# Values of units 1 and 2 in one pass of 512 columns, branch A's last gate group between units 2 and 3, the mixing's products on GpSimd

## The chip, the cores and the metric

The kernel runs on one core of a Trainium2 chip. The metric is the device time of one execution in microseconds (us). The kernel before takes 898.06 us, the median of three runs (897.68 to 898.46).

## What is computed

One layer of a hybrid decoder on a sequence of 512 tokens with 2048 features, then a final RMSNorm, in fp32.

```python
def reference(x, c, norm_g, w_ada, b_ada, w_in, ln_v_g, ln_v_b, w_s, b_s, b_f, w_out, final_g):
    cond = jax.nn.silu(c)
    ...
        shift, scale, gate = jnp.split(mod, 3, axis=-1)
        h = rms_norm(x, norm_g[l]) * (1.0 + scale[:, None, :]) + shift[:, None, :]
        z = h @ w_in[l]
        u_a, v_a, g_a, q_b, k_b, v_b, g_b, f_b = jnp.split(z, pts, axis=-1)
        y_a = chunked_spatial_gating(jax.nn.gelu(u_a, approximate=False),
                                     jax.nn.gelu(v_a, approximate=False),
                                     ln_v_g[l], ln_v_b[l], w_s[l], b_s[l]) * jax.nn.silu(g_a)
        y_b = forgetting_attention(q_b, k_b, v_b, f_b, b_f[l]) * jax.nn.silu(g_b)
        y = jnp.concatenate([y_a, y_b], axis=-1) @ w_out[l]
        x = x + gate[:, None, :] * y
    return rms_norm(x, final_g)
```

`z` has 7184 columns: 1024 each for u, v and gate of branch A and for q, k, v and gate of branch B, and 16 forget logits. Branch A normalises v and mixes it over the tokens: 8 heads, each with a lower triangular 128x128 matrix on chunks of 128 tokens. Branch B is causal attention of 16 heads of 64, whose scores have the running sum of log-sigmoid forget gates added.

## The kernel before

**Engines.** PE (TensorE) multiplies; DVE (VectorE), ACT (ScalarE) and POOL (GpSimd) do the rest; SP issues most loads. A framework orders each engine's instructions ahead of time, from the order of the code and from priorities; each engine then runs its own list strictly in order and waits on semaphores. A wait therefore holds up all that is queued behind it.

**Products.** Every fp32 operand is split into a high and a low part, and a product is three matmuls: high by high, low by high, high by low. Weights come in tiles (`w_tile`, L126 to L146): SP loads `raw` (4 buffers), ACT copies it to the high part `whi` (L141), DVE subtracts for the low part `wlo` (L145; 2 buffers each). Two forms of product use them:

- `mm_cols` (L163 to L165): 128 weight columns are stationary and 512 tokens move; used by q, k and the gates (`col_group`, L177). Names: q, k, ga (gates of A), gb (gates of B).
- `mm_toks` (L173 to L175): 128 tokens are stationary and the weight columns move; used by the values, va of branch A (512 columns at a time) and vb of branch B. `v_group` (L825) does one unit's 256 columns (272 in unit 0, with the forget logits).

**Units.** Branch B's heads are done in four units of four heads. Order of groups: va, ga (the last 256 columns of A's gates), v0, q0, k0, gb0, q1, k1, v1, gb2, q2, k2, v2, q3, k3, v3, gb1, gb3, then the output projection. A unit's values go to the tile `vs` as high and low parts right behind its pass (L66 on ACT, L67 on DVE).

**Ticks.** After each weight tile, `tick()` (L148) takes one entry of the list `slots` (branch A's mixing, then attention) and one of `fillers` (mostly `gate_step`, the output gate's products on POOL, L723 and L727). So the small work is spread among the matmuls by counting weight tiles. A unit's attention is eight slots: scores (2 slots), `lse`, then exps and products with the values.

- Scores (L589, L590) are matmuls; DVE adds the mask and takes the minimum (L591), ACT exponentiates (L595).
- `lse` (L602 to L613): ACT takes the logarithm, PE transposes (L607), ACT copies the result to `lt` (L609), SP writes it by four small copies into rows of the q tiles (L612). Then `pins.append([4, rows_in])`: the load of the fifth weight tile from there is issued only behind those copies. This tile is called the pinned tile below.
- `probs`: matmuls t (L629, L630), exps p on ACT (L633, with a table load ahead), split into pth (ACT, L66) and ptl (DVE, L67). `values`: matmuls o (L645) and evacuation (L653 to L655).

**Branch A's mixing.** `norm_half` (L885) normalises and splits va for four heads; `mix_head` (L898 to L919) mixes one head: eight matmuls into two banks (L907, L908), four `scalar_tensor_tensor` (STT below) on DVE into `mt` (L911, L916), and the product of `mt` with y (L919, on DVE). `evac_g` (L445) multiplies in A's gates (L442, L451). The list of slots: norm 0; mix 0, 1; mix 2, 3; norm 1; then mix 4, 5, 6, 7 one by one. The first four slots fall into ga, the others into v0.

**PSUM.** Banks of the kind "mm" (four) take the groups' sums; "x" takes turns on four more banks, for scores, t, o, mixing, transposes, and q0's two sums.

Of the kernel before, what the change touches and what calls it, by code (L numbers as in the profile page):

```python
# [23 lines left out]
U0, V0, G0, Q0, K0, VB0, GB0, F0 = 0, 1024, 2048, 3072, 4096, 5120, 6144, 7168  # L24
# [3 lines left out]
def trunk_kernel(  # L28
# [17 lines left out]
    nc = tc.nc  # L46
# [6 lines left out]
    act = ctx.enter_context(tc.tile_pool(name="act", bufs=KB))  # L53
# [5 lines left out]
    def bank(tag, name):  # L59
        if tag == "x":  # L60
            tag = "bbbc"[turn[0] % 4]
            turn[0] += 1
        return ps.tile([P, 512], F32, tag=tag, name=name, bufs={"mm": 4, "b": 3, "c": 1}[tag])

    def split(hi, lo, src, eng=None):
        a = nc.scalar.activation(hi, src, AF.Copy)  # L66
        return a, (eng or nc.vector).tensor_tensor(lo, src, hi.bitcast(F32), ALU.subtract)  # L67
# [193 lines left out]
    def ada_sums(q, i, ga):  # L261
# [5 lines left out]
        for j in range(2):  # L267
# [15 lines left out]
            else:  # L283
                for c_ in ((slice(0, P), slice(P, 2 * P)) if q == 0 and kk == KB - 2 else (slice(0, 256),)):
# [153 lines left out]
    y = [None] * KB  # L438

    def silu2(dst, pt):  # L440
        ta = nc.scalar.activation(dst, pt, AF.Tanh, scale=0.5)
        nc.vector.scalar_tensor_tensor(dst, dst, 1.0, pt, ALU.add, ALU.mult)  # L442
        return ta

    def new_y(b):  # L445
        y[b] = act.tile([P, S], F32, tag="ya" if b < 8 else "yb", bufs=8, name=f"y{b}")

    def evac_g(b, pt, pool):
        sg = pool.tile([P, S], F32, name=f"sgA{b}", tag="sgB", bufs=3 if pool is st else 4)
        ta = silu2(sg, pt)  # L450
        nc.vector.scalar_tensor_tensor(y[b], sg, 0.5, y[b], ALU.mult, ALU.mult)  # L451
        return ta

    for q, (k0, nk) in enumerate(CH):
# [10 lines left out]
        for si, sid in enumerate(order):  # L465
# [50 lines left out]
    pb = ctx.enter_context(tc.tile_pool(name="pb", bufs=1))  # L516
# [14 lines left out]
    vs_ = []  # L531
# [4 lines left out]
    def halves(e):  # L536
        return (slice(0, 64), slice(64, 128)) if e == 0 else (slice(64, 128), slice(0, 64))
# [257 lines left out]
    def spatial_weights():  # L795
# [10 lines left out]
        for i in range(2):  # L806
# [11 lines left out]
            for j in range(4):  # L818
# [3 lines left out]
                    bias2[:, h, :], ALU.mult, ALU.add,  # L822
                )

    def v_group(u):  # L825
        c0 = u * 256
        banks = [bank("mm", f"vb{u}_{t}") for t in range(NT)]
        segs, nk = ([(VB0 + c0, 256)], 4) if u else ([(VB0, 256), (F0, 16)], 2)
        w = sum(z for _, z in segs)
        for k in range(0, KB, nk):  # L830
            hi, lo = w_tile(segs, k, nk, name=f"vb{u}_{k}")
            mm_toks(banks, w, hi, lo, hh, hl, list(range(k, k + nk)), 0, KB - 1)
            tick()
        with tc.high_priority(offset=EPRI):
            for t in range(NT):
                src = banks[t][:, 0:256].rearrange("p (i d) -> p i d", d=64)
                for e in range(2):
                    a, o = halves(e)
                    split(vs_[0][:, t, e::2, a], vs_[0][:, t, e::2, o], src[:, e::2, :])
# [22 lines left out]
    c_ = lambda f, *a: (lambda: f(*a))  # L862
# [32 lines left out]
    def mix_head(h):  # L895
        g, j = divmod(h, 4)
        hs = slice(h * P, (h + 1) * P)
        js = slice(j * P, (j + 1) * P)  # L898
        mt = pb.tile([P, 512], F32, name=f"mt{h}", tag="p", bufs=2)
        b2 = bias2[:, h, :]  # L900
        w2 = wsp[h // 4][:, h % 4].rearrange("p a t -> p (a t)")
        for n in range(2):
            mx = bank("x", f"mix{h}_{n}")
            for i in range(2):
                vh, vl = vhl[2 * n + i, g]
                o = mx[:, i * 256 : (i + 1) * 256]
                nc.tensor.matmul(o, vh[:, js], w2, start=True, stop=False)  # L907
                nc.tensor.matmul(o[:, 0:P], vl[:, js], w2[:, 0:P], start=False, stop=True)  # L908
            m3 = mx.rearrange("p (n a t) -> p n a t", n=2, a=2)
            o3 = mt[:, n * 256 : (n + 1) * 256].rearrange("p (n t) -> p n t", n=2)  # L910
            nc.vector.scalar_tensor_tensor(  # L911
                o3, m3[:, :, 0, :], lngb[:, h : h + 1],
                bass.AP(tensor=b2.tensor, offset=b2.offset, ap=[b2.ap[0], [0, 2], b2.ap[1]]),
                ALU.mult, ALU.add,
            )
            nc.vector.scalar_tensor_tensor(  # L916
                o3, m3[:, :, 1, :], lngb[:, h : h + 1], o3, ALU.mult, ALU.add
            )
        nc.vector.tensor_tensor(y[h], y[h], mt, ALU.mult)  # L919

    fillers.append(spatial_weights)
    for k in range(8):
        fillers.extend([lambda k=k: sum_step(0, k), lambda: None])
    va_products()
    slots.extend([
        [c_(norm_half, 0)],
        [c_(mix_head, 0), c_(mix_head, 1)],
        [c_(mix_head, 2), c_(mix_head, 3)],
        [c_(norm_half, 1)],
        [c_(mix_head, 4)], [c_(mix_head, 5)], [c_(mix_head, 6)], [c_(mix_head, 7)],  # L930
    ])
    col_group([(G0 + 768, 256)], [(lambda pt, b=b: evac_g(b, pt, pb)) for b in range(6, 8)], "ga")
    vs_.append(pb.tile([P, NT, 4, P], F32R, name="vs", tag="vs"))
    v_group(0)
    heads_tiles()
# [17 lines left out]
    fillers.append(lambda: [f() for f in late_stores])  # L953
    qk_group(0)
    g_group(0)
    for u in range(1, 4):
        if u == 2:
            g_group(2)
        qk_group(u)
        v_group(u)  # L960

# [61 lines left out]
    def wtile(name):  # L1023
        return wp.tile([P, 2, 512], F32, tag="raw", name=name, bufs=4)
# [85 lines left out]
    def unit(u):  # L1110
# [3 lines left out]
        def w_raw(half, g, name):  # L1114
            return lambda i: wsplit(wget(wtile(f"{name}_{u}_{i}"), half, g, i), f"{name}_{u}_{i}")
# [6 lines left out]
            return f  # L1122

        def tiles(n, tag, b=2):
            pool = act if tag == "yb" else pb
            return [pool.tile([P, S], F32, name=f"{n}{u}_{t}", tag=tag, bufs=b) for t in range(2)]

        def evac(f):
# [6 lines left out]
                f(t)  # L1135

        product(V, "A11", w_raw(1, g1, "p1"), True)
        c1 = tiles("c1", "yb", 8) if u else tiles("c1", "th")
        evac(lambda t: nc.scalar.activation(c1[t], V[t], AF.Copy))
        Z = [bank("mm" if u else "x", f"woZ{u}_{t}") for t in range(2)]  # L1140
        product(Z, "S3", w_sum(1, "p7"), True)
        c7 = tiles("c7", "yb", 8) if u else tiles("c7", "p")
        evac(lambda t: nc.scalar.activation(c7[t], Z[t], AF.Copy))
        X = [bank("x", f"woX{u}_{t}") for t in range(2)]
        product(X, "S2", w_sum(3, "p6"), True)
        if u:
# [128 lines left out]
```

## Time and profile before

| | |
|---|---|
| median of three runs | 898.06 us (897.68 to 898.46) |
| the profiled execution | 899.12 us |
| its span in the trace | 897.4 us |
| granted clock of TensorE | 0.997 of full speed |
| PE, DVE, ACT, POOL busy | 98%, 68%, 50%, 53% of the span |

Where the groups start on PE, in us of the span: va 189.6, ga 279.4, v0 305.0, q0 333.5, k0 356.1, gb0 378.2, q1 405.1, k1 432.8, v1 461.3, gb2 493.5, q2 520.1, k2 547.5, v2 569.7, q3 598.6, k3 626.8, v3 653.0, gb1 681.7; the output projection runs from 735 to the end.

In rows of the timeline the first number is the start, the second the duration in us (both from the first instruction to the last of a group that stands under one row, with its count as x), then engine, line, operation, and out<-in; in brackets is the idle time of the engine just before, and what ended it. PE's matmuls are pipelined: a 512-column one lasts 0.39 us and the next starts 0.23 us after it, so steps from start to start tell PE's speed. In a table of stretches a row has the stretch, its length, busy time with the number of instructions of PE, PE's weight load, DVE, ACT and POOL, the granted clock, the DMA share and GB/s.

### The profile page before, as it was taken

The numbers are of one execution on the slowest core, as the hardware profiler recorded it, in microseconds if no ns is written. First come the engines' busy times: TensorE is split into PE (matmuls) and PEld (weight loads), VectorE is DVE, ScalarE is ACT, GpSimd is POOL, SyncE is SP. The second block draws the span as 40 slices with busy tenths as digits, with TensorE's granted clock in tenths as the row PEclk, the third lists the DMA queues.
The fourth block names the chain that finished last, engine by engine and source line by source line (L and its number), as shares of the span: only waits on it lengthen the run. The fifth ranks groups of instructions, "written<-read, shape, count | busy, mean of one in ns | idle before, by whom it ended". The sixth has DMA issues, their size and how long they took to land.

```text
span 897.4 us, 12688 instructions
## 1 busy us (share of the span) xinstructions
PE 881.7 (98%) x4453; PEld 744.7 (83%) x4453; DVE 614.7 (68%) x999; ACT 444.4 (50%) x778; POOL 479.7 (53%) x407
## 2 busy tenths in 40 slices
PE   9999999999999999999999999999999999999995
PEld 6788888887888897887889888998898888888884
DVE  5878888374427967563876664547664779997686
ACT  6653333452224224564656554556466567654454
POOL 1266554515676269999799779957566520000001
PEclk9999999999999999999999999999999999999998
DMA  9999996348986275544443536466666466577575
GB/s 340 354 352 355 354 344 205 111 134 284 331 285 200 61 212 155 156 139 136 142 150 117 187 107 188 129 193 198 222 188 211 165 214 200 174 263 244 178 245 195
DMA packets 123216, 188.91 MB, mean 211 GB/s; under 512 B 9856, under 2 KB 86864, under 8 KB 122640
## 3 DMA queue, kind: packets, MB, share of 16 engines
q1 hardware_dynamic: 113248, 153.97, 53.6%
q0 software_dynamic: 9472, 33.56, 11.6%
q8 instruction: 35, 0.57, 0.3%
q10 hardware_dynamic: 432, 0.57, 0.2%
q14 instruction: 29, 0.24, 0.1%
HBM read 166.90 MB, written 20.97 MB: 209 GB/s over the span
## 4 chain that ended last, share of the span: by engine, by line
PE 89%; DMA 4%; DVE 3%; ACT 1%; issue 1%; SPq 1%; POOLq 0%; POOL 0%; ACTq 0%
PE s L163 6%; PE s L165 6%; PE s L164 6%; PE k L165 3%; PE gb L164 3%; PE gb L165 3%; PE gb L163 3%; PE k L164 3%; PE k L163 3%; PE vb L173 3%; PE vb L174 3%; PE va L175 3%; PE va L174 3%; PE va L173 3%; PE vb L175 3%; PE q L165 3%
## 5 line engine op out<-in xcount | busy, mean ns | idle before, releaser
L723 POOL TENSOR_SCALAR gate<-gate,sc 128x512 f32<-128x512 f32 x64 | 108.5, 1708 | 1.4
L727 POOL TENSOR_TENSOR gate<-gate,gate 128x512 f32<-128x512 f32 x60 | 91.1, 1518 | 2.4
L145 POOL TENSOR_TENSOR wlo_st<-raw_st,whi_st 128x768 fp32r<-128x768 f32 (+3 forms) x33 | 66.0, 2001 | 45.0 <-ACT whi_st L141 39.8
L163 PE MATMUL s<-hh,whi_st 128*128 128x512 f32 x224 | 86.2, 391 | 0.9 <-ACT sp L501 0.9
L164 PE MATMUL s<-hl,whi_st 128*128 128x512 f32 x224 | 86.2, 389 | 0.0
L66 ACT ACTIVATE whi_p<-p 128x1024 fp32r<-128x1024 f32 x52 | 55.2, 1061 | 57.2 <-PE woZ L1059 22.1
L1102 POOL TENSOR_TENSOR sfin<-sfin,nhalf 128x1 f32<-128x1 f32 x2 | 1.5, 746 | 149.6 <-DVE sfin L1194 149.6
L285 DVE SCALAR_TENSOR_TENSOR acc<-ada,sc,acc 128x512 f32<-128x512 f32 x98 | 73.9, 754 | 6.2 <-DMA ada<-in_w_ada_dram 3.4
L67 DVE TENSOR_TENSOR wlo_p<-p,whi_p 128x1024 fp32r<-128x1024 f32 x52 | 63.4, 1221 | 19.6 <-ACT whi_p L66 19.5
L165 PE MATMUL s<-hh,wlo_st 128*128 128x512 f32 x224 | 75.3, 391 | 0.0
L173 PE MATMUL vb<-whi_vb,hh 128*128 128x256 f32 (+1 forms) x256 | 72.3, 285 | 0.8 <-DVE sgA L442 0.5
L174 PE MATMUL vb<-whi_vb,hl 128*128 128x256 f32 (+1 forms) x256 | 72.3, 285 | 0.0
L175 PE MATMUL vb<-wlo_vb,hh 128*128 128x256 f32 (+1 forms) x256 | 70.7, 284 | 0.0
L141 ACT ACTIVATE whi_st<-raw_st 128x768 fp32r<-128x768 f32 (+3 forms) x35 | 31.1, 890 | 68.6 <-PE s L164 49.3
L775 POOL TENSOR_TENSOR ts<-ts 128x256 f32<-128x256 f32 x64 | 57.0, 903 | 13.2 <-DMA ts<-in_w_out_dram 11.4
L67 DVE TENSOR_TENSOR ptl<-p,pth 128x512 fp32r<-128x512 f32 (+1 forms) x64 | 45.4, 733 | 14.1 <-ACT pth L66 13.0
L145 DVE TENSOR_TENSOR wlo_va<-raw_va,whi_va 128x1024 fp32r<-128x1024 f32 x16 | 24.6, 1538 | 39.3 <-ACT whi_va L141 39.3
L163 PEld LDWEIGHTS s<-hh,whi_st 128*128 128x128 f32 x224 | 42.0, 188 | 10.2 <-ACT sp L501 1.7
L163 PE MATMUL k<-hh,whi_k 128*128 128x512 f32 x128 | 50.4, 394 | 0.0
L163 PE MATMUL q<-hh,whi_q 128*128 128x512 f32 x128 | 50.4, 394 | 0.0
L164 PE MATMUL q<-hl,whi_q 128*128 128x512 f32 x128 | 50.4, 394 | 0.0
L173 PE MATMUL va<-whi_va,hh 128*128 128x512 f32 x128 | 50.3, 393 | 0.0
(317 smaller groups left out, 2628.0 us busy)
## 6 DMA issues: line engine op xcount, KB each, us to landing
ada<-in_w_ada_dram SPq DMA_DIRECT2D x128, 256.0 KB
gate<-in_w_ada_dram POOLq DMA_DIRECT2D x32, 512.0 KB, 4.4
p<-ts SPq DMA_DIRECT2D x32, 512.0 KB
p<-in_w_out_dram SPq DMA_DIRECT2D x24, 512.0 KB
raw_st<-in_w_in_dram SPq DMA_DIRECT2D x22, 384.0 KB
raw_va<-in_w_in_dram SPq DMA_DIRECT2D x16, 512.0 KB
raw_q<-in_w_in_dram SPq DMA_DIRECT2D x16, 512.0 KB
raw_k<-in_w_in_dram SPq DMA_DIRECT2D x16, 512.0 KB
```

The source lines that it names most:

```text
L67: return a, (eng or nc.vector).tensor_tensor(lo, src, hi.bitcast(F32), ALU.subtract)
L145: (loeng or nc.vector).tensor_tensor(lo, raw, hi.bitcast(F32), ALU.subtract)
L163: nc.tensor.matmul(pt, hi[:, j, cs], hh[k], start=(k == first), stop=False)
L164: nc.tensor.matmul(pt, hi[:, j, cs], hl[k], start=False, stop=False)
L165: newest = nc.tensor.matmul(pt, lo[:, j, cs], hh[k], start=False, stop=(k == last))
L173: nc.tensor.matmul(o, ah[k][:, tsl], hi[:, j, :], start=(k == first), stop=False)
L174: nc.tensor.matmul(o, al[k][:, tsl], hi[:, j, :], start=False, stop=False)
L175: nc.tensor.matmul(o, ah[k][:, tsl], lo[:, j, :], start=False, stop=(k == last))
L285: nc.vector.scalar_tensor_tensor((sb if kk == KB - 1 else a)[:, :, c_], ga[:, j, :, c_], col, a[:, :, c_], ALU.mult, ALU.add,)
L723: nc.gpsimd.tensor_scalar(ga[:, j] if kk else a, ga[:, j], sc[:, kk : kk + 1], None, ALU.mult)
L727: done = nc.gpsimd.tensor_tensor(a, a, ga[:, j], ALU.add)
L775: done = nc.gpsimd.tensor_tensor(dst, l, r, ALU.subtract)
```

## The change

Three edits, and the buffers that they need.

- **One pass of 512 columns.** `v_group(1)` loads the value columns of units 1 and 2 together, in 8 tiles of two row blocks each. Unit 1's half is split to `vs` as before; unit 2's half goes by ACT to two SBUF tiles `v2`, and `v_group(2)` only splits from those. Of the pools, y and the like lose two of eight buffers of the kind "yb" to a new kind "yc".
- **Gate group moved.** ga no longer stands ahead of v0 but between unit 2's values and q3. The list of the mixing is packed into v0's eight tiles. The groups' order becomes va, v0, q0, k0, gb0, v1 (with unit 2), q1, k1, gb2, q2, k2, ga, q3, k3, v3, gb1, gb3.
- **Products on GpSimd.** `y[h] * mt` goes from DVE (L919 before) to POOL (L940 after).

```diff
@@ v_group
+    def v_split(t, src):
+        src = src.rearrange("p (i d) -> p i d", d=64)
+        for e in range(2):
+            a, o = halves(e)
+            split(vs_[0][:, t, e::2, a], vs_[0][:, t, e::2, o], src[:, e::2, :])
...
+        if u == 2:
+            for t in range(NT):
+                v_split(t, v2[t // 2][:, t % 2 * 256 : t % 2 * 256 + 256])
+            return
         banks = [bank("mm", f"vb{u}_{t}") for t in range(NT)]
-        segs, nk = ([(VB0 + c0, 256)], 4) if u else ([(VB0, 256), (F0, 16)], 2)
+        segs, nk = {
+            0: ([(VB0, 256), (F0, 16)], 2), 1: ([(VB0 + c0, 512)], 2), 3: ([(VB0 + c0, 256)], 4),
+        }[u]
...
+                if u == 1:
+                    nc.scalar.activation(
+                        v2[t // 2][:, t % 2 * 256 : t % 2 * 256 + 256], banks[t][:, 256:512], AF.Copy
+                    )
@@ mix_head
-        nc.vector.tensor_tensor(y[h], y[h], mt, ALU.mult)
+        nc.gpsimd.tensor_tensor(y[h], y[h], mt, ALU.mult)
@@ slots
         [c_(norm_half, 0)],
-        [c_(mix_head, 0), c_(mix_head, 1)],
-        [c_(mix_head, 2), c_(mix_head, 3)],
-        [c_(norm_half, 1)],
-        [c_(mix_head, 4)], [c_(mix_head, 5)], [c_(mix_head, 6)], [c_(mix_head, 7)],
+        [c_(mix_head, 0)], [c_(mix_head, 1), c_(norm_half, 1)],
+        [c_(mix_head, 2), c_(mix_head, 3)], [c_(mix_head, 4)], [c_(mix_head, 5)], [c_(mix_head, 6)],
+        [c_(mix_head, 7)],
     ])
-    col_group([(G0 + 768, 256)], [(lambda pt, b=b: evac_g(b, pt, pb)) for b in range(6, 8)], "ga")
@@ the groups
     g_group(0)
-    for u in range(1, 4):
-        if u == 2:
-            g_group(2)
-        qk_group(u)
-        v_group(u)
+    v_group(1)
+    qk_group(1)
+    g_group(2)
+    qk_group(2)
+    v_group(2)
+    col_group([(G0 + 768, 256)], [(lambda pt, b=b: evac_g(b, pt, pb)) for b in range(6, 8)], "ga")
+    qk_group(3)
+    v_group(3)
```

Line numbers of the kernel after are higher: by 3 ahead of `v_group`, by 21 in the mixing. The attention slots of units 0 to 3 fall into gb0 and q1, v1 and gb2, v2 and q3, v3 and gb1 before; now into gb0 and v1, gb2 and q2, ga and q3, v3 and gb1.

The end of v0 on PE, before: the last matmuls of v0 (vb0_3, its tile 14), and the first of q0.

```order
L173 MATMUL vb0_3_2785<-whi_vb0_14_3070,hh15_1687 128x272
L174 MATMUL vb0_3_2785<-whi_vb0_14_3070,hl15_1688 128x272
L175 MATMUL vb0_3_2785<-wlo_vb0_14_3071,hh15_1687 128x272
L163 MATMUL q0_0_3150<-hh0_386,whi_q0_0_3154 128x512
L164 MATMUL q0_0_3150<-hl0_387,whi_q0_0_3154 128x512
```

The same place now. mix4_1 to mix7_1 are banks of the mixing of heads 4 to 7, and vh and vl the parts of va.

```order
L175 MATMUL vb0_3_2551<-wlo_vb0_14_2925,hh15_1687 128x272
L929 MATMUL mix4_1_2819<-wsp1_1892,vl3_1_2714 128x128
L929 MATMUL mix5_1_2866<-wsp1_1892,vl3_1_2714 128x128
L928 MATMUL mix6_0_2906<-wsp1_1892,vh0_1_2698 128x256
...
L929 MATMUL mix7_1_2960<-wsp1_1892,vl3_1_2714 128x128
L163 MATMUL q0_0_3020<-hh0_386,whi_q0_0_3024 128x512
```

The last piece of heads 4 and 5 and all of heads 6 and 7 stand between v0 and q0 (16 matmuls from mix6_0 to mix7_1). The banks take turns, and q0_0 gets mix6_0's.

DVE at that place, before: the parts of the values (vs) and the low parts of q0's weights.

```order
L145 TENSOR_TENSOR wlo_q0_0_3155<-raw_q0_0_3152,whi_q0_0_3154 128x1024
L67 TENSOR_TENSOR vs_2781<-vb0_0_2782,vs_2781 128x2x64
L67 TENSOR_TENSOR vs_2781<-vb0_1_2783,vs_2781 128x2x64
L67 TENSOR_TENSOR vs_2781<-vb0_2_2784,vs_2781 128x2x64
L67 TENSOR_TENSOR vs_2781<-vb0_0_2782,vs_2781 128x2x64
L145 TENSOR_TENSOR wlo_q0_4_3219<-raw_q0_4_3216,whi_q0_4_3218 128x1024
```

Now, from the first STT that reads mix4_1 (one more split of values stands behind it, and an STT of mix5_1) to the one that reads mix6_0 for the second time:

```order
L932 SCALAR_TENSOR_TENSOR mt5_2858<-mix5_1_2866,cols_128,bias2_1904 128x256
L937 SCALAR_TENSOR_TENSOR mt4_2811<-mix4_1_2819,cols_128,mt4_2811 128x256
L145 TENSOR_TENSOR wlo_q0_4_3089<-raw_q0_4_3086,whi_q0_4_3088 128x1024
L937 SCALAR_TENSOR_TENSOR mt5_2858<-mix5_1_2866,cols_128,mt5_2858 128x256
L67 TENSOR_TENSOR vs_2547<-vb0_3_2551,vs_2547 128x2x64
L67 TENSOR_TENSOR vs_2547<-vb0_1_2549,vs_2547 128x2x64
L67 TENSOR_TENSOR vs_2547<-vb0_2_2550,vs_2547 128x2x64
L932 SCALAR_TENSOR_TENSOR mt6_2905<-mix6_0_2906,cols_128,bias2_1904 128x256
L932 SCALAR_TENSOR_TENSOR mt6_2905<-mix6_1_2913,cols_128,bias2_1904 128x256
L67 TENSOR_TENSOR vs_2547<-vb0_3_2551,vs_2547 128x2x64
L937 SCALAR_TENSOR_TENSOR mt6_2905<-mix6_0_2906,cols_128,mt6_2905 128x256
```

With the two rows ahead of these (the STT of mix4_1 and a split of vb0_0) they are 13 instructions: 7 STTs, 5 splits, 1 wlo.

ACT at unit 1's lse, before: whi_gb2_8 is a plain tile, p4 are the exps of the unit's first head.

```order
L609 ACTIVATE lt1_4535<-lse1_4530 32x128
L66 ACTIVATE vs_2781<-vb1_3_4271 128x2x64
L141 ACTIVATE whi_gb2_8_4825<-raw_gb2_8_4823 128x1024
L633 ACT_TABLE_LOAD
L633 ACTIVATE p4_0_4606<-t4_0_4602 128x512
```

Now whi_q2_12 stands there, of the pinned tile:

```order
L141 ACTIVATE whi_q2_8_4897<-raw_q2_8_4895 128x1024
L612 ACTIVATE lt1_4643<-lse1_4638 32x128
L141 ACTIVATE whi_q2_12_4978<-raw_q2_12_4976 128x1024
L636 ACT_TABLE_LOAD
L636 ACTIVATE p4_0_4691<-t4_0_4687 128x512
```

In unit 2 whi_q3_12 stands at the same point now. In unit 0 before, it was whi_q1_12, the pinned tile too; now a plain one, whi_vb1_4, stands there.

More of the change, by code (lines that the diff above doesn't have):

```diff
@@ L288, in ada_sums, with ytag @@
                     )
+    def ytag(b):
+        return {"tag": "ya", "bufs": 8} if b < 8 else {"tag": "yb", "bufs": 6} if b < 14 else {"tag": "yc", "bufs": 2}
     xT = []
@@ L414, in trunk_kernel @@
                 turn_x(kb, t)
-        xk = act.tile([P, S], F32, tag="ya" if kb < 8 else "yb", bufs=8, name=f"xT{kb}")
+        xk = act.tile([P, S], F32, name=f"xT{kb}", **ytag(kb))
         nc.scalar.activation(xk, tps[kb], AF.Copy)
@@ L445, in new_y @@
     def new_y(b):
-        y[b] = act.tile([P, S], F32, tag="ya" if b < 8 else "yb", bufs=8, name=f"y{b}")
+        y[b] = act.tile([P, S], F32, name=f"y{b}", **ytag(b))
     def evac_g(b, pt, pool):
@@ L823, in spatial_weights @@
                 )
+    v2 = []
+    def v_split(t, src):
[3 more added lines that the diff above has]
+            split(vs_[0][:, t, e::2, a], vs_[0][:, t, e::2, o], src[:, e::2, :])
     def v_group(u):
         c0 = u * 256
+        if u == 2:
+            for t in range(NT):
+                v_split(t, v2[t // 2][:, t % 2 * 256 : t % 2 * 256 + 256])
+            return
         banks = [bank("mm", f"vb{u}_{t}") for t in range(NT)]
-        segs, nk = ([(VB0 + c0, 256)], 4) if u else ([(VB0, 256), (F0, 16)], 2)
+        segs, nk = {
+            0: ([(VB0, 256), (F0, 16)], 2), 1: ([(VB0 + c0, 512)], 2), 3: ([(VB0 + c0, 256)], 4),
+        }[u]
         w = sum(z for _, z in segs)
@@ L833, in v_group @@
             tick()
+        if u == 1:
+            v2.extend([act.tile([P, S], F32, name=f"v2_{z}", tag="yc", bufs=2) for z in range(2)])
         with tc.high_priority(offset=EPRI):
             for t in range(NT):
[L836 to L839, printed above, removed]
+                v_split(t, banks[t][:, 0:256])
                 if u == 0:
                     nc.scalar.activation(ft[:, t, :], banks[t][:, 256:272], AF.Copy)
+                if u == 1:
+                    nc.scalar.activation(
+                        v2[t // 2][:, t % 2 * 256 : t % 2 * 256 + 256], banks[t][:, 256:512], AF.Copy
+                    )
         if u == 0:
@@ L1124, in tiles @@
         def tiles(n, tag, b=2):
-            pool = act if tag == "yb" else pb
+            pool = act if tag in ("yb", "yc") else pb
             return [pool.tile([P, S], F32, name=f"{n}{u}_{t}", tag=tag, bufs=b) for t in range(2)]
@@ L1137, in unit @@
         product(V, "A11", w_raw(1, g1, "p1"), True)
-        c1 = tiles("c1", "yb", 8) if u else tiles("c1", "th")
+        c1 = tiles("c1", "yb", 6) if u else tiles("c1", "th")
         evac(lambda t: nc.scalar.activation(c1[t], V[t], AF.Copy))
@@ L1141, in unit @@
         product(Z, "S3", w_sum(1, "p7"), True)
-        c7 = tiles("c7", "yb", 8) if u else tiles("c7", "p")
+        c7 = tiles("c7", "yc", 2) if u else tiles("c7", "p")
         evac(lambda t: nc.scalar.activation(c7[t], Z[t], AF.Copy))
@@ L1149, in unit @@
         else:
-            u2, u3 = tiles("u2", "yb", 8), tiles("u3", "yb", 8)
+            u2, u3 = tiles("u2", "yb", 6), tiles("u3", "yb", 6)
         evac(lambda t: nc.vector.tensor_tensor(u2[t], X[t], c1[t], ALU.add))
```

## Prediction

> **What bounds the kernel now.** First the page: its span, its engines, and the shares of the chain that ended last.
>
> ```profile
> span 897.4 us, 12688 instructions
> PE 881.7 (98%) x4453; PEld 744.7 (83%) x4453; DVE 614.7 (68%) x999; ACT 444.4 (50%) x778; POOL 479.7 (53%) x407
> PE 89%; DMA 4%; DVE 3%; ACT 1%; issue 1%; SPq 1%; POOLq 0%; POOL 0%; ACTq 0%
> ```
>
> PE is busy 98% of the span. So the time moves in two ways only: PE gets less work, or PE stands still less or more. Work on the other engines counts only where PE waits for it. Next the list of PE's own waits from 285 to 700 us, the part that the change touches (us in total, times, longest).
>
> ```profile
> PE o L645 <- ACT pth L66: 1.5, 1, 1.5
> PE vb L173 <- DVE sgA L442: 0.5, 1, 0.5
> PE s L589 <- DVE tm L655: 0.3, 1, 0.3
> PE vb L173 <- DVE k L570: 0.3, 1, 0.3
> ```
>
> Those are all the long waits there: one in unit 0's attention, one in v0, and two short ones. There is little to win in waits and much room to lose. The table of stretches places the attention (PE busy is the second figure): k0 to q1's end first, then v1, then v2.
>
> ```profile
> 405.10:432.80 27.70, 26.22 (x123) 21.54 (x122) 11.64 (x22) 14.94 (x27) 21.77 (x18) 1.00 0.49 153
> 461.25:493.50 32.25, 31.49 (x235) 29.45 (x234) 23.37 (x53) 22.24 (x57) 30.09 (x22) 1.00 0.43 129
> 569.70:598.60 28.90, 28.90 (x230) 28.37 (x229) 19.09 (x47) 20.05 (x52) 21.87 (x23) 1.00 0.44 138
> ```
>
> PE idles 1.5 us in q1 and 0.8 in v1, and nothing in v2; the granted clock is 1.00 throughout, so it takes no part in the sum.
>
> **1. The pass of 512 columns.** PE's rows in two stretches without other work (v2, and branch A's values), and the group of the narrow form:
>
> ```profile
> 587.11 0.28 PE L173 MATMUL vb<-whi_vb,hh 128*128 128x256 f32 x1
> ...
> 587.59 0.28 PE L174 MATMUL vb<-whi_vb,hl 128*128 128x256 f32 x1
> ```
> ```profile
> 229.99 0.39 PE L174 MATMUL va<-whi_va,hl 128*128 128x512 f32 x1
> ...
> 231.12 0.39 PE L174 MATMUL va<-whi_va,hl 128*128 128x512 f32 x1
> ```
> ```profile
> L173 PE MATMUL vb<-whi_vb,hh 128*128 128x256 f32 x192 | 54.1, 283 | 0.3 <-DVE k L570 0.3
> ```
>
> Durations overlap, so starts count: four steps of 256 columns take 0.48 us (0.12 each), five of 512 take 1.13 (0.226). The group has 64 matmuls for each of units 1, 2 and 3, on each of three lines; two units are 2 x 3 x 64 = 384 matmuls, 46.1 us. In their place come 192 of 512 columns, 43.4 to 43.6 us. **-2.5 us**, certain, as the path is PE's. All else that PE does is moved, not changed. [...]
>
> The splits of unit 2 now read SBUF copies: four more ACT evacuations of 128x256 and no PE work. I cost them at nothing (ACT is 50% busy) except where they fall among the softmax, in point 4.
>
> **2. Branch A's mixing moved into v0; the product on GpSimd.** What goes is a wait in v0:
>
> ```profile
> 301.97 3.81 POOL L67 TENSOR_TENSOR vl<-va,vh 128x512 fp32r<-128x512 f32 x3
> 302.03 4.91 DVE L919 TENSOR_TENSOR y<-y,mt 128x512 f32<-128x512 f32 x2
> 307.59 0.39 PE L173 MATMUL vb<-whi_vb,hh 128*128 128x272 f32 x1 [0.55 <-DVE sgA L442]
> 311.83 0.69 DVE L919 TENSOR_TENSOR y<-y,mt 128x512 f32<-128x512 f32 x1
> ```
>
> Two products took 4.91 us beside POOL's 3.81, and one alone 0.69; the gate evacuation behind them was late, and PE stood 0.55 idle and 0.71 more than its step. The gate group is elsewhere now: **-0.7**.
>
> What comes is at the end of v0. All eight heads now mix in v0's eight tiles, so heads 6 and 7 fall behind its last matmul. q0's two banks come out of the same rotation as the mixing's: q0's first matmul waits until DVE has read mix6 for the second time (the STT of L937). By the order, DVE has 13 instructions between the last matmul of v0 and that point: 7 STTs, 5 splits of values, 1 wlo_q. Their rows before, and the mixing's on PE:
>
> ```profile
> 317.21 0.94 DVE L911 SCALAR_TENSOR_TENSOR mt<-mix,cols,bias 128x256 f32<-128x256 f32 x2 [0.92 <-PE mix L908]
> 318.70 0.87 DVE L916 SCALAR_TENSOR_TENSOR mt<-mix,cols,mt 128x256 f32<-128x256 f32 x2
> 334.67 2.25 DVE L145 TENSOR_TENSOR wlo_q<-raw_q,whi_q 128x1024 fp32r<-128x1024 f32 x1 [0.68 <-ACT whi_q L141]
> 336.85 1.11 DVE L67 TENSOR_TENSOR vs<-vb,vs 128x128 fp32r<-128x128 f32 x4
> 340.06 1.23 DVE L145 TENSOR_TENSOR wlo_q<-raw_q,whi_q 128x1024 fp32r<-128x1024 f32 x1 [2.10 <-ACT whi_q L141]
> ```
> ```profile
> 306.48 0.28 PE L907 MATMUL mix<-wsp,vh 128*128 128x256 f32 x1
> ...
> 306.82 0.22 PE L908 MATMUL mix<-wsp,vl 128*128 128x128 f32 x1
> ```
>
> At 0.40 to 0.44 a STT, 0.23 to 0.28 a split and 1.23 the wlo_q the chain is 5.2 to 5.7 us. PE has meanwhile only sixteen mixing matmuls, four of which step 0.34 us from first to last start: 1.6 us. PE stands 3.6 to 4.1 us; **+3.9**. If the wlo_q runs beside a GpSimd product it takes 2.25, as at 334.67, and the wait is 5.1; nothing in the order shortens the chain, so 3.5 is the lower end. [...]
>
> The GpSimd products delay GpSimd's own queue: y6 and y7 stand behind two gate steps there, and the forget gates' DVE and ACT work waits for them (its tiles are the same buffers).
>
> ```profile
> 346.99 3.34 DVE L691 RECIPROCAL f<-f 16x512 f32<-16x512 f32 x1 [0.65 <-ACT f L689]
> 350.25 1.15 DVE L145 TENSOR_TENSOR wlo_q<-raw_q,whi_q 128x1024 fp32r<-128x1024 f32 x1
> ```
>
> q0's last wlo_q stands behind that reciprocal and is just in time now; later by 0.1 to 1.5: **+0.6**.
>
> **3. Gate group moved.** Its matmuls cost the same. Its place is kept for the attention slots of unit 2, so this counts in point 4.
>
> **4. The attention slots.** All move by 4 to 8 tiles of weights. The wait that the list shows, unit 0's, row by row:
>
> ```profile
> 412.93 0.27 PE L607 MATMUL lse<-ident,n 128*32 128x128 f32 x1
> 413.53 2.74 SPq L612 DMA_DIRECT2D q<-lt  x4
> 416.37 0.37 SPq L135 DMA_DIRECT2D raw_q<-in_w_in_dram  x1
> 421.58 1.06 ACT L141 ACTIVATE whi_q<-raw_q 128x1024 fp32r<-128x1024 f32 x1 [8.08 <-DMA raw_q<-in_w_in_dram]
> 422.66 1.28 ACT L633 ACT_TABLE_LOAD   x1
> 423.95 0.98 ACT L633 ACTIVATE p<-t 128x512 f32<-128x512 f32 x2
> 424.82 1.04 ACT L66 ACTIVATE pth<-p 128x512 fp32r<-128x512 f32 x2
> 425.50 0.50 PE L645 MATMUL o<-pth,vs 128*128 128x512 f32 x1 [1.48 <-ACT pth L66]
> ```
>
> The pinned weight tile is loaded only behind the four row copies, and ACT stands 8.08 us at its whi; the exps, and so PE, are queued behind. The exps' first result came 12.57 us after the lse transpose. In unit 1 the tile ahead of the exps was another, long landed:
>
> ```profile
> 499.11 1.06 ACT L141 ACTIVATE whi_gb<-raw_gb 128x1024 fp32r<-128x1024 f32 x1 [3.47 <-PE gb L164]
> 500.19 1.28 ACT L633 ACT_TABLE_LOAD   x1
> 502.35 1.04 ACT L66 ACTIVATE pth<-p 128x512 fp32r<-128x512 f32 x2
> ```
>
> By the order the pinned tile stands ahead of the exps now in units 1 and 2, and no longer in unit 0. Unit 0's wait goes: **-1.6** (1.48 and what its step lost). For the others I take unit 0's times from lse: whi ready at 9.7 us (421.58 + 1.06 - 412.93), first exps done by 11.6 and 12.0. Unit 1: PE has 10.5 us of matmuls by their steps, then wants a bank that an exp frees (1.1 late), and 0.2 follows: **+1.3**. Unit 2: PE has 8.1 us until it needs that whi itself, 1.6 late; four matmuls later (0.9) it needs a bank of the second exp, ready at 12.0: 1.4 more; **+3.0**. Unit 0's small waits at the end of k1 and in v1 (the rest of the idle time in the stretches) go, and units 2 and 3 end beside evacuations of the gate group and of v3: **+0.5**, between -1 and 2.
>
> **The sum**: -2.5 - 0.7 + 3.9 + 0.6 - 1.6 + 1.3 + 3.0 + 0.5 = +4.5 us. The profiled run took 899.12 us, 1.7 beyond its span and 1.06 above the median of 898.06; the sum goes on both alike: 902.6 against the median (903.6 in the profiled state).
>
> **Rivals.**
> A. The pinned loads land 1.6 us sooner or more than unit 0's did, since the tile is asked for in a quieter stretch. Then units 1 and 2 cost nothing: -2.5 - 0.7 + 3.9 + 0.6 - 1.6 = -0.3, 897.8, no change. For it: unit 0's load took 5 us from issue. Against: of the 8.65 us from lse to whi's start (412.93 to 421.58) the row copies alone are 3.4, and they stay.
> B. Faster: as A, and the attention's small waits go as well (-1.2), with chain and forget at their lower ends (3.5 and 0.1): -2.4, 895.7. It decides at a whi ready 8.1 us behind lse in unit 2. For it: units 1 to 3 now cost PE next to nothing. Against: the order itself.
> C. Slower still: GpSimd's products hold DVE in the chain (+1.2) and in the forget work (+0.9), and the tails reach 2 us (+1.5): +8.1, 906.2. For it: 4.91 us above; against: only one two-input DVE operation stands in the chain.
>
> **How the numbers follow.** Forecast 0.48, A 0.16, B 0.21, C 0.15. A timing of this kernel tells about 0.2%, 1.8 us, from no change, so A is "same", B faster, forecast and C slower; 0.02 of the forecast's lower edge goes to same: 0.21, 0.18, 0.61. The range goes from B, 895.7, to C, 906.2, which leaves out some of B and C beyond.
>
> **What would show it.** Right: PE idle 3.5 us or more between the last mix and the first q matmul, behind DVE mt; ACT at whi_q 8 us in units 1 and 2, with PE waiting there, and none in unit 0. Wrong: PE's rows without that gap, or whi_q done 8 us behind lse, or 512-column steps above 0.24 us.

## The result and the profile after

The changed kernel takes 907.25 us, the median of four runs (905.48 to 908.35), against 898.07 (897.68 to 898.46): 1.0093 times the time before, 95% interval 1.0079 to 1.0108. It is 9.2 us slower. The sign was forecast; the size was twice the forecast and 1 us outside the range.

The profiled execution took 906.60 us, 7.5 more than that of before. The page's first lines:

```profile
span 904.8 us, 12295 instructions
PE 884.4 (98%) x4261; PEld 738.7 (82%) x4261; DVE 612.9 (68%) x991; ACT 446.2 (49%) x782; POOL 491.7 (54%) x415
PE 73%; POOL 11%; DVE 6%; DMA 5%; issue 3%; ACT 2%; SPq 1%; POOLq 0%; ACTq 0%; DVEq 0%
```

PE has 192 matmuls fewer and yet is busy 2.7 us longer: a busy engine that has become slower is the first thing to look into. The list of PE's waits from 275 to 720 us:

```profile
PE q L163 <- ACT whi_q L141: 2.5, 1, 2.5
PE q L163 <- DVE mt L937: 1.6, 1, 1.6
PE mix L928 <- DVE mt L937: 1.5, 2, 0.9
PE vb L175 <- DVE wlo_vb L145: 1.2, 1, 1.2
PE t L632 <- ACT p L636: 0.7, 1, 0.7
PE k L163 <- ACT whi_k L141: 0.6, 1, 0.6
```

Three places make up nearly all of it: one in v0 (wlo_vb), the end of v0 (mt twice at the mixing and once at q0), and unit 2's slots in q3 (whi_q, then an exp).

**v0.** DVE, POOL and PE in v0's second half:

```profile
302.17 4.85 DVE L145 TENSOR_TENSOR wlo_vb<-raw_vb,whi_vb 128x544 fp32r<-128x544 f32 x1 [1.07 <-ACT whi_vb L141]
```
```profile
301.39 1.31 POOL L67 TENSOR_TENSOR vl<-va,vh 128x512 fp32r<-128x512 f32 x1
302.65 1.30 POOL L940 TENSOR_TENSOR y<-y,mt 128x512 f32<-128x512 f32 x1
303.89 2.53 POOL L67 TENSOR_TENSOR vl<-va,vh 128x512 fp32r<-128x512 f32 x2
```
```profile
307.07 0.39 PE L175 MATMUL vb<-wlo_vb,hh 128*128 128x272 f32 x1 [1.19 <-DVE wlo_vb L145]
```

The same kind of low part, alone, in the trace of before:

```profile
328.20 0.72 DVE L145 TENSOR_TENSOR wlo_vb<-raw_vb,whi_vb 128x544 fp32r<-128x544 f32 x1 [2.26 <-ACT whi_vb L141]
```

What took 0.72 us there took 4.85 here. It began while POOL was at a low part of va, and ended at 307.0, 0.6 us behind the end of POOL's two-input work at 306.4. PE's next start was 1.4 us late.

**The end of v0.** PE's rows, with their idle time:

```profile
312.29 0.36 PE L928 MATMUL mix<-wsp,vh 128*128 128x256 f32 x1 [0.61 <-DVE mt L937]
...
313.82 0.35 PE L928 MATMUL mix<-wsp,vh 128*128 128x256 f32 x1 [0.87 <-DVE mt L937]
...
316.05 0.47 PE L163 MATMUL q<-hh,whi_q 128*128 128x512 f32 x1 [1.58 <-DVE mt L937]
...
317.39 0.63 PE L164 MATMUL q<-hl,whi_q 128*128 128x512 f32 x1
317.81 0.63 PE L165 MATMUL q<-hh,wlo_q 128*128 128x512 f32 x1
```

Over their steps those starts are 0.78, 1.04 and 1.75 us late, 3.6 together, each behind DVE's second reading of a mixing bank. The last two rows show something that the kernel before did not have there: a 512-column step of 0.42 us, where 0.23 is usual. PE is busy, at half speed. The table of stretches of 2 us there (the third figure from the end is the granted clock):

```profile
314.00:316.00 2.00, 0.47 (x4) 0.31 (x3) 1.82 (x7) 0.65 (x4) 2.00 (x5) 1.00 0.77 206
316.00:318.00 2.00, 1.95 (x6) 1.61 (x7) 0.75 (x3) 0.00 (x0) 1.94 (x3) 0.66 0.16 56
318.00:320.00 2.00, 2.00 (x7) 1.54 (x6) 1.21 (x4) 0.00 (x0) 1.91 (x3) 0.50 0.21 70
320.00:322.00 2.00, 2.00 (x10) 1.67 (x9) 0.00 (x0) 0.00 (x0) 2.00 (x3) 0.99 0.93 272
```

The clock was granted at a half for about 3.4 us right behind the wait: (0.34 + 0.50 + 0.01) x 2 = 1.7 us lost.

**Unit 2.** ACT at its lse, and PE in q3:

```profile
609.17 0.27 ACT L612 ACTIVATE lt<-lse 32x128 fp32r<-32x128 f32 x1 [2.62 <-PE lse L610]
618.71 1.06 ACT L141 ACTIVATE whi_q<-raw_q 128x1024 fp32r<-128x1024 f32 x1 [9.27 <-DMA raw_q<-in_w_in_dram]
```
```profile
612.37 0.39 SPq L135 DMA_DIRECT2D raw_q<-in_w_in_dram  x1
```
```profile
619.82 0.50 PE L163 MATMUL q<-hh,whi_q 128*128 128x512 f32 x1 [2.47 <-ACT whi_q L141]
...
622.11 0.79 PE L632 MATMUL t<-q,k 128*128 128x512 f32 x1 [0.72 <-ACT p L636]
```
```profile
620.00:622.00 2.00, 1.39 (x4) 0.59 (x4) 1.03 (x1) 1.99 (x4) 2.00 (x2) 0.61 0.57 185
622.00:624.00 2.00, 1.89 (x5) 1.50 (x6) 1.39 (x4) 2.00 (x5) 0.29 (x1) 0.50 0.89 223
624.00:626.00 2.00, 2.00 (x6) 1.61 (x5) 1.73 (x3) 1.26 (x5) 0.00 (x0) 0.50 0.78 309
626.00:628.00 2.00, 2.00 (x7) 1.58 (x7) 0.00 (x0) 0.68 (x2) 1.16 (x2) 0.69 0.77 214
```

The pinned tile's whi starts 9.8 us behind the lse transpose (608.87), PE's starts are 2.6, 1.1 and 0.4 us late, and the clock drops again: at most 3.4 us lost (0.39 + 0.50 + 0.50 + 0.31, times 2). Waits and clock overlap by about 1 us here: all that PE's starts are late from 619.5 to 628 us is 6.5 us.

Summed over all starts of PE's rows from 300 us to the end of the input projection, what they are late beyond the step of their size is 8.8 us before and 18.1 after. By place: v0's second half to k0's end 1.8 and 8.2; unit 0's slots and what is beside them 4.7 and 1.4; unit 1's 1.3 and 1.1; units 2 and 3 1.0 and 7.5. So +9.3, less the 2.5 of the columns, +6.8, of the 7.5 between the two profiled executions. The remaining 0.7 is not placed to the tenth: va starts 0.2 us later, and the output projection comes 0.7 us later behind the last gates.

### The profile page after: what moved, and what is told of

Its sections match the earlier page's. It is cut to its first block, busy times and chain, and to the rows that moved or that the text cites. A ratio compares the mean times of both kernels' runs of the same rounds, so it can differ in the third digit from the quotient of the medians.

```text
span 904.8 us, 12295 instructions
## 1 busy us (share of the span) xinstructions
PE 884.4 (98%) x4261; PEld 738.7 (82%) x4261; DVE 612.9 (68%) x991; ACT 446.2 (49%) x782; POOL 491.7 (54%) x415
## 4 chain that ended last, share of the span: by engine, by line
PE 73%; POOL 11%; DVE 6%; DMA 5%; issue 3%; ACT 2%; SPq 1%; POOLq 0%; ACTq 0%; DVEq 0%
PE s L163 6%; PE s L164 6%; PE s L165 6%; POOL gate L726 5%; POOL gate L730 4%; PE va L175 3%; PE va L174 3%; PE va L173 3%; PE vb L175 3%; PE vb L173 3%; PE vb L174 3%; PE gb L163 2%; PE gb L164 2%; PE gb L165 2%; PE k L165 2%
## 5 line engine op out<-in xcount | busy, mean ns | idle before, releaser
L726 POOL TENSOR_SCALAR gate<-gate,sc 128x512 f32<-128x512 f32 x64 | 114.3, 1796 | 1.5
L730 POOL TENSOR_TENSOR gate<-gate,gate 128x512 f32<-128x512 f32 x60 | 89.2, 1487 | 2.3
L778 POOL TENSOR_TENSOR ts<-ts 128x256 f32<-128x256 f32 x64 | 54.1, 858 | 16.2 <-DMA ts<-in_w_out_dram 14.7
L174 PE MATMUL vb<-whi_vb,hl 128*128 128x272 f32 (+2 forms) x192 | 61.5, 322 | 0.0
L173 PE MATMUL vb<-whi_vb,hh 128*128 128x272 f32 (+2 forms) x192 | 60.9, 322 | 0.0
L175 PE MATMUL vb<-wlo_vb,hh 128*128 128x272 f32 (+2 forms) x192 | 58.9, 323 | 1.2 <-DVE wlo_vb L145 1.2
L165 PE MATMUL q<-hh,wlo_q 128*128 128x512 f32 x128 | 50.9, 407 | 0.0
L163 PE MATMUL gb<-hh,whi_gb 128*128 128x512 f32 x128 | 50.1, 392 | 0.0
```

Source lines behind the costliest of these rows:

```text
L163: nc.tensor.matmul(pt, hi[:, j, cs], hh[k], start=(k == first), stop=False)
L165: newest = nc.tensor.matmul(pt, lo[:, j, cs], hh[k], start=False, stop=(k == last))
L173: nc.tensor.matmul(o, ah[k][:, tsl], hi[:, j, :], start=(k == first), stop=False)
L174: nc.tensor.matmul(o, al[k][:, tsl], hi[:, j, :], start=False, stop=False)
L175: nc.tensor.matmul(o, ah[k][:, tsl], lo[:, j, :], start=False, stop=(k == last))
L726: nc.gpsimd.tensor_scalar(ga[:, j] if kk else a, ga[:, j], sc[:, kk : kk + 1], None, ALU.mult)
```

## The experiments

Theory: three places where PE waits, and the slower clock that two of these waits bring, make the time. Rivals: the product on GpSimd by itself; the attention slots, wherever they fall; the slow clock coming by itself. All ratios are to the kernel before on the same chip.

**The product back on DVE.**

```diff
-        nc.gpsimd.tensor_tensor(y[h], y[h], mt, ALU.mult)
+        nc.vector.tensor_tensor(y[h], y[h], mt, ALU.mult)
```

> The kernel after with the mixing's product back on DVE; all else as after. Theory (the time comes from three waits of PE and from the slower clock behind two of them): the 1.4 us wait in v0, where one wlo_vb took 4.85 us on DVE beside GpSimd's work, shrinks, but DVE has two products of 0.7 more in the chain at the end of v0, so that wait grows; unit 2 is untouched. In all between -1.5 and +1 us against 907.3, so 905.8 to 908.3. Rival (the product on GpSimd is what slows the kernel, by holding DVE): 5 us or more come back, 902 or less.

905.06 us, ratio 1.0056 (1.0037 to 1.0074), where the changed kernel had 1.0093. PE's waits:

```profile
PE q L163 <- DVE mt L937: 4.1, 1, 4.1
PE q L163 <- ACT whi_q L141: 2.6, 1, 2.6
PE t L632 <- ACT p L636: 1.1, 1, 1.1
PE k L163 <- ACT whi_k L141: 0.4, 1, 0.4
```

The wait at wlo_vb is gone, so it was the work on GpSimd beside it; the wait ahead of q0 is one of 4.1 now. The clock was low for longer, 6.8 us, of which 1.3 lie inside the wait (2.7 us lost, not 1.7), so the trace is no shorter. The medians say more: against the kernel before on the same chip (899.41) it is 5.6 us slower, not 9.2. Some 3.5 us came back, more than the theory's 1.5 and less than the rival's 5, and the trace does not show where.

**Unit 2's row copies pinned one tile later.**

```diff
-            pins.append([4, rows_in])
+            pins.append([5 if u == 2 else 4, rows_in])
```

> The kernel after, but unit 2's row copies are pinned to the sixth following weight tile, not the fifth, so that whi_q3_12 is loaded ahead of them. Theory: unit 2's waits of 2.6 and 1.1 us go, and with them the stretch behind at half the granted clock, which cost another 3 us: -6 to -7 us, 900 to 901. Rival (the slow clock there has another cause and comes by itself): only the 4 us of waits, 903. Rival (the load is late as the DMA queues are full, whatever it waits for): no change, 907.

903.67 us, 1.0059 (1.0030 to 1.0088), with single runs from 900.5 to 911.3. In the trace unit 2's waits and its slow clock are both gone; PE's list has only the rows of v0, q0 and k0. PE's starts are 6.5 us less late in all than in the changed kernel's trace. So the low clock there does not come by itself: it left with the wait. Against the kernel before on the same chip less of it is seen, 4 to 5 us in the medians and 2 to 3 in the ratios (counted from the repeat or from the first measurement), partly since the changed kernel doesn't always wait so long there (the repeat, below). Three of its ten runs took over 908 us, and what they lost wasn't seen.

**q0's sums in the other banks.**

```diff
-        col_group([(Q0 + c0, 256)], [evac_q(2 * u), evac_q(2 * u + 1)], f"q{u}", "mm" if u else "x")
+        col_group([(Q0 + c0, 256)], [evac_q(2 * u), evac_q(2 * u + 1)], f"q{u}", "mm")
```

> The kernel after with q0's two sums in the other set of banks (mm), so that q0 no longer waits for DVE's second reading of mix6. Theory: the wait of 1.75 us ahead of q0 goes or becomes a wait for the values' evacuation of under 1 us; the two ahead of mix7 (0.8 and 1.0) stay; the clock stays at 1.0 if the idle time in that stretch falls clearly, which is worth 1.7: -1.5 to -3.5 us. The scheduler also puts unit 2's first exps ahead of whi_q3_12 here, which takes away the second of its waits (1.1); so in all 902.5 to 905.5. Rival (DVE's chain is the limit, not the bank): the wait reappears in q0 at its wlo or in the forget gates' stretch, 906 to 907.

912.55 us, 1.0139 (1.0106 to 1.0172): slower, a miss in the total. At the place in question it did what was expected: PE's starts from 300 to 325 us are late by 2.7 us, not 6.9, the wait ahead of q0 is gone, and the clock stays at 1.00. But the scheduler laid out the rest anew, and PE waits in other places:

```profile
PE q L163 <- ACT whi_q L141: 3.0, 1, 3.0
PE o L648 <- DVE ptl L67: 2.7, 2, 1.8
PE q L163 <- ACT v L860: 1.8, 1, 1.8
```

with the clock low behind three such waits (5.1 us lost). One edit moved the whole schedule.

**The product on GpSimd alone, in the kernel before.** The first edit above, the other way round.

> The kernel before with only the mixing's product moved to GpSimd. Theory: the 0.7 us wait in v0 goes or moves, the rest is as before: 897 to 898.5. Rival (the product on GpSimd holds DVE for long and costs by itself): 901 or more.

900.18 us, 1.0005 (0.9991 to 1.0018). The time is the same, but the trace does not show the product to be free. DVE is held in v0 here as well. The stretch from 308 to 310 us (DVE is the fourth figure, POOL the sixth):

```profile
308.00:310.00 2.00, 2.00 (x18) 1.96 (x17) 2.00 (x1) 1.14 (x2) 2.00 (x2) 1.00 0.01 4
```

One operation of DVE fills all of it, with POOL busy throughout; those of the kernel before that stand in v0 behind POOL's work (306.9 to 313.2 us) took 0.72 us at most. In the kernel before two products took 4.91 us beside POOL's at the same place and PE waited 0.5, so little changed: PE waits 0.6 us for a wlo_vb here and 0.8 for a wlo_q in q0. In return unit 0's wait of 1.5 us is one of 0.4, as its pinned whi came 7.1 us behind the lse transpose, not 8.65.

**The gate group back ahead of v0; the pass alone; the pass alone with later pins.** The group and the list of slots as before; then the product on DVE as well; then pins of 5.

```diff
     v_group(2)
-    col_group([(G0 + 768, 256)], [(lambda pt, b=b: evac_g(b, pt, pb)) for b in range(6, 8)], "ga")
```

> The kernel after with branch A's last gate group back ahead of v0 and the mixing's list as before: the 512-column pass and the product on GpSimd stay. Theory: the waits between v0 and q0 (3.6 us) and in v0 (1.4, but the kernel before had 0.7) go, with the 1.7 us of slower clock; in unit 2 the pinned tile is whi_k3_12 now, which PE wants later than whi_q3_12, so most of the 4.1 us of waits and the 3.4 of slower clock go too. What is left against the kernel before are the 2.5 us of columns and unit 0's waits: -2 to -5 us against before. Rival (the moved attention slots cost wherever they fall): within 1 us of before or slower.

> The kernel before with the 512-column pass alone (product on DVE, gate group ahead of v0). Theory: as the run with the gate group back, within 1 us of it: -2 to -5 us against before. Where the product matters (rival), this is 1.5 us or more better than that run.

> The 512-column pass alone, with the row copies of all units pinned to the sixth following weight tile instead of the fifth. Theory: what is left of PE's waits for exps behind a pinned tile goes: 0 to -2 us against the run with the pass alone, 893 to 896 where before takes 898. Rival (the pinned tile no longer costs where PE has over 12 us of work behind lse): no difference.

912.71 us (1.0139), 921.42 (1.0231) and 917.65 (1.0191). None of the forecasts held, and these runs tell little of the pass: without the gate group there are four weight tiles too few between k2 and q3, and the second half of unit 2's attention reads the q and k of unit 3. So they do not compute the same layer, and PE waits up to 9.8 us for the tiles of unit 3's q. What they show is why the gate group was moved: not for its own sake, but to give unit 2's slots their four ticks.

**The kernel before with later pins.**

```diff
-            pins.append([4, rows_in])
+            pins.append([5, rows_in])
```

> The kernel before with the row copies pinned to the sixth following tile. Theory: unit 0's wait of 1.5 us, in which PE and ACT stand behind whi_q1_12, goes: -1 to -2 us against before. Rival (the load lands late whatever it waits for): no difference.

897.46 us, 0.9985 (0.9970 to 1.0000). The list of PE's waits from 200 us on has one row left:

```profile
PE vb L173 <- DVE sgA L442: 0.5, 1, 0.5
```

The mechanism of unit 0's wait in the prediction is right: it is the pin. The whi of that tile now starts 3.7 us behind the lse transpose.

**The changed kernel once more.**

> The changed kernel itself once more, on the chip of the runs beside it. The ratio to before stays 1.008 to 1.011. If the theory of the clock holds, the trace shows again a stretch at half the granted clock behind the wait ahead of q0 and another behind unit 2's wait, each costing 1.7 us or twice that; the rival (the slow clock came by itself) has it elsewhere or nowhere.

907.05 us, 1.0078 (1.0056 to 1.0100). Its profiled execution was the fastest of the four, 904.28. Ahead of q0 there is the same wait and again 1.7 us of clock. In unit 2, however:

```profile
611.76 0.27 ACT L612 ACTIVATE lt<-lse 32x128 fp32r<-32x128 f32 x1 [2.38 <-PE lse L610]
618.65 1.06 ACT L141 ACTIVATE whi_q<-raw_q 128x1024 fp32r<-128x1024 f32 x1 [6.62 <-DMA raw_q<-in_w_in_dram]
```
```profile
PE t L632 <- ACT p L636: 1.1, 1, 1.1
```

Counted from the lse transpose, the same tile came 2.7 us sooner than in the first trace (7.2 us, not 9.8), PE waited 1.1 us, and the clock stayed at 1.00. The same program, with and without the low clock, and with and without a long wait ahead of it: the clock follows the wait.

**The pass with another group moved.** Branch B's first gate group in the place of branch A's; product on DVE; pins of 5.

```diff
     qk_group(0)
-    g_group(0)
     v_group(1)
...
     v_group(2)
+    g_group(0)
     qk_group(3)
```

> The 512-column pass with branch A's last gate group left ahead of v0 and the product on DVE; the four weight tiles that the attention slots of unit 2 need come from branch B's first gate group instead, which moves from behind k0 to behind unit 2's values; row copies pinned to the sixth tile. Theory: no wait of 3.6 us ahead of q0 and no slow clock there; none behind a pinned tile; unit 0's slots now all fall into the pass of 512, and its last values come right at the end of it, which may cost a wait of 1 to 2 us at the start of q1. In all -2 to -5 us against before, 894 to 897 where before takes 898 to 899. Rival (a wide pass costs by itself, by its bank or its splits from SBUF copies): at or above before.

906.98 us, 1.0085 (1.0068 to 1.0102): a miss. No wait ahead of q0 and a clock of 1.00 there, as expected, but unit 0's eight slots in one pass cost far more than the 1 to 2 us allowed for:

```profile
PE o L648 <- ACT pth L66: 3.7, 4, 1.7
PE gp L792 <- ACT p L636: 2.3, 1, 2.3
PE q L163 <- ACT v L860: 1.5, 1, 1.5
```

and the clock was at a half for two stretches of 6.8 us in and behind them.

**The mixing's list one tile shorter.** Unit 2's pins of 5 as well; product on DVE, and on GpSimd.

```diff
-        [c_(mix_head, 0)], [c_(mix_head, 1), c_(norm_half, 1)],
-        [c_(mix_head, 2), c_(mix_head, 3)], [c_(mix_head, 4)], [c_(mix_head, 5)], [c_(mix_head, 6)],
-        [c_(mix_head, 7)],
+        [c_(mix_head, 0), c_(norm_half, 1)], [c_(mix_head, 1), c_(mix_head, 2)],
+        [c_(mix_head, 3), c_(mix_head, 4)], [c_(mix_head, 5)], [c_(mix_head, 6)], [c_(mix_head, 7)], [],
```

> The kernel after with three edits: product on DVE, unit 2's row copies pinned to the sixth tile, and the mixing's list one tile shorter, so that only head 7's matmuls are behind v0's last one. Theory: the wait ahead of q0 falls from 4.3 us (run with the product on DVE) to 1 or 2, too short for the clock to drop, and unit 2's waits and its slow clock go: 6 to 7 us off each place, 891 to 894, faster than both kernels. Rival (DVE has no more room in v0, so the earlier mixing only moves the wait into v0): 898 to 901.

> As the run with the shorter list, but with the product on GpSimd. Theory: a wlo_vb on DVE stands beside GpSimd's products and low parts again, and PE waits for it in v0 by 1 to 2 us: that much slower than the run with the product on DVE. Rival (the product on GpSimd is free): the same time, or faster by the 5.5 us of DVE work that it takes away.

900.89 us (1.0024, 1.0008 to 1.0041) and 901.54 (1.0048, 1.0020 to 1.0076). Unit 2 is clean in both, but the wait ahead of q0 stays as it was, 4.1 us with the product on DVE, with a stretch of 6.8 us at half the clock that begins inside it. PE only has fewer matmuls left to do meanwhile. So with the product on DVE no wait of 1 or 2 us came about there, and this run does not show whether one is too short for the clock to drop. The rival held: DVE is busy for 19.9 of the 21 us from 295 to 316. In the second, the medians differ by less than the 1 to 2 us expected, and its profiled execution (911.72, far above its median) has a wait of another kind, 5.3 us behind a POOL memset of unit 3's q that stood in POOL's queue behind its transfers of the output projection's weights, and again 6.8 us at half the clock from inside that wait.

**Bank and product crossed.** Pins of 6 in all three; q0's sums in mm with the product on GpSimd; in mm with the product on DVE; in the old banks with the product on DVE.

> The kernel after with q0's sums in the banks of the values (mm) and the row copies of all units pinned to the seventh following tile; product on GpSimd. Theory: the wait ahead of q0 and the slow clock behind it go (in the run with the banks alone the stretch from 300 to 325 us lost 2.5 us, not 6.9), but the wait at the wlo_vb beside GpSimd (1.4) and one at mix7 (0.8) stay; unit 2's wait and its slow clock go. 897 to 900 where before takes 898 to 899. Rival (what follows in k0 and unit 0 gets late by the same time): 902 or more.

> As the run before it in this list, with the product on DVE. Theory: the wait at wlo_vb in v0 goes (1.4); the chain of DVE in front of the values' evacuation is 2 us longer, and q0 waits for that, in its banks or at its weights, by up to 2 us. 896 to 900, and faster than before if no wait over 2 us is left. Rival (a bank wait of 4.3 us was only the sign of DVE's own lateness): a wait of 3 us or more stands again in q0 or its forget gates, 901 or more.

> As the run with the product on DVE, but q0's sums in the old banks: bank and pin told apart. Theory: the wait of 4.3 us ahead of q0 and 3.4 us of slow clock behind it stay, as in the other run with the product on DVE; unit 2 is clean: 900 to 901, 4 to 6 us slower than with q0 in the other banks. Rival (bank does not matter): within 1 us of it.

| | time, us | ratio to before |
|---|---|---|
| mm, GpSimd | 901.04 | 1.0015 (1.0002 to 1.0028) |
| mm, DVE | 896.13 | 0.9966 (0.9952 to 0.9981) |
| old banks, DVE | 907.83 | 1.0104 (1.0076 to 1.0132) |

The first list is of q0 in mm with the product on DVE, the second with the old banks:

```profile
PE k L165 <- DVE wlo_k L145: 0.9, 2, 0.8
PE k L163 <- ACT whi_k L141: 0.5, 1, 0.5
PE q L163 <- ACT ft L858: 0.4, 1, 0.4
PE vb L173 <- DVE k L573: 0.3, 1, 0.3
```
```profile
PE q L163 <- DVE mt L937: 4.1, 1, 4.1
PE k L165 <- DVE wlo_k L145: 0.9, 2, 0.5
PE k L163 <- ACT whi_k L141: 0.6, 1, 0.6
PE t L633 <- DMA q<-lt: 0.5, 1, 0.5
```

With the old banks q0 waits 4.1 us for DVE, in the others 0.4; the waits in k0, 1.4 and 1.5 us, stand in both. So the wait is the bank that q0 takes over from mix6, and not DVE's lateness as such. The fourth combination, the old banks with the product on GpSimd at these pins, was not run. The bank run with the product on DVE beats both kernels: 2.4 us under the kernel before, about what the columns save. The product on GpSimd costs 4.9 us at the same banks and pins. Its trace has the waits of 1.2 at wlo_vb and 0.6 at the mixing, one of 1.7 at k0's wlo, where the other has 0.9, and one of 1.9 ahead of q1. The gap between the banks, 11.7 us, is more than the profiled execution of the slower run shows (903.67, with 4.3 of wait and 1.7 of clock at q0); its other runs are at 907 to 910, and what they lose beyond that wasn't seen. So the two profiled executions, 898.76 and 903.67, bear the bank out with 4.9 us, and the rest of the gap is open.

## Why the prediction was wrong, step by step

- **Columns, -2.5:** right. The 192 steps of 512 columns in the new pass have a median of 0.227 us, 43.6 in all.
- **The wait in v0, -0.7:** it went, and one of 1.4 at a wlo_vb came in the same group. How it came about, a DVE operation that lasts longer beside GpSimd's work (a wlo_vb of 4.85 us, 0.72 alone), stood in the prediction, priced for the chain and the forget gates' work alone (rival C); eight wlo_vb stand in v0.
- **Ahead of q0, +3.9:** right in mechanism and size (3.6; 4.3 with the product on DVE). But only 1.75 of the 3.6 stand at q0; the other 1.8 come earlier, where heads 6 and 7 wait for banks of the mixing itself, which the prediction did not have. That the bank is the releaser is shown by the crossed runs: with the product on DVE, 4.1 us of wait ahead of q0 in the old banks, 0.4 in mm.
- **Forget gates, +0.6:** about right: 1.3 us of late starts from 325 us to the end of k0, against 1.0 before.
- **Unit 0, -1.6, and small waits:** too low; 3.3 us went. (The first row of the prediction's table of stretches is q1 alone.)
- **Unit 1, +1.3:** wrong; next to nothing. Its pinned whi came 7.4 us behind lse (531.54), 1.3 sooner than the 8.65 of the sum, which is most of the way to rival A.
- **Unit 2, +3.0:** right in place and mechanism; up to 4.1 us in one trace (about 1 of it shared with the slow clock), 1.3 in another. The step took one landing time, 8.65 us, for all; in the tiles of units 1 and 2, in two executions, it was 7.2 to 9.8.
- **The clock:** the step that failed. The prediction said that the granted clock, being 1.00 throughout, takes no part in the sum. That reads a clock that was measured with short waits into a kernel with longer ones. Behind the waits that were themselves forecast, the clock was at a half for 3.4 and 6.8 us in the profiled run, 1.7 and up to 3.4 us lost. Add these 5.1 us to the forecast of 902.6 and it is 907.7, where 907.25 was measured. That this comes so near is partly luck: the two profiled executions differ by 7.5 us, which leaves 2.4 without the clock, where the sum had 4.5. So the other terms were some 2 us too high together, mostly in units 0 and 1, in spite of the 1.4 that came in v0; and in the repeat, profiled at 904.28, the clock lost 1.7 us in all at these places.

That long waits bring the low clock is shown by pairs: the same program in unit 2 with a wait of 2.5 us (6.8 us at half the clock) and with one of 1.1 (none), and the pinned run, with no wait there and no low clock. The other traces bear it out. In the 17 traces there are 24 stretches at half the clock between 190 us and the end of the matmuls; each begins inside a wait of PE or at most 1.5 us behind the end of one of 1.6 us or more, and each wait of 2 us or more has one. By the tables of 2 us they last 3.3 to 3.4 us, 6.7 to 6.8 or, once, 10.2. A wait need not be as long as the stretch behind it: waits of 1.8 to 2.6 us brought the low clock here.

## What to carry to other kernels

Where PE is 98% busy, as here, price a new wait of 2 us or more as the wait and the low clock with it: the stretches of 3.4 and 6.8 us at a half lost 1.7 and up to 3.4 us. Waits of 1.5 us and less, far apart, cost only themselves here (1.5 in unit 0 before, 1.1 in unit 2 of the repeat, the clock at 1.00 behind both), and those between came out both ways. When work is packed ahead of a group, look at which bank that group takes over and from whom: with the bank changed, and the late DVE work the same, q0 waited 0.4 us, not 4.1. And the place of a group can matter for what is tied to it: the moved gate group carried four attention slots of unit 2.

## What was not expected of the hardware

The clock fell to a half behind a wait of 1.8 us in one place (q0 in mm with the early pins, at 582 us), and not behind one of 1.9 us in another (mm with GpSimd, at 445 us) or 1.5 (at 425 us before): below 2 us no fixed length decides here. In 15 of the 17 profiled executions, all but those of the kernel before and of the changed kernel with the product back on DVE, it is also low for 3.4 or 6.8 us within the first 40 us, and the work just ahead of va ends up to 3.6 us later (POOL's last low part at 187.0 us in the fastest variant, 183.3 before). The kernel before's own runs spread by as much, 897.7 to 902.5 us over all sessions: those with a mean clock of 0.992 took 900.5 to 902.5, those with 0.997 took 897.9 to 899.1. And one operation of DVE lasted over several of GpSimd's in turn: the wlo_vb of 4.85 us, 0.72 alone, stood beside four of them, from 302.2 to 307.0 us, and ended 0.6 us behind the last.
